# Column mean of 8192 x 8192 floats: first load ahead of the critical section, stores behind it, GpSimd as its leader

## Chip, cores and metric

The kernel runs on one core of one Trainium2 chip. The metric is the device time of one execution in microseconds (us). The core has TensorE (PE), VectorE (DVE), ScalarE (ACT), GpSimd (POOL) and SyncE (SP), each with its own queue of instructions, and 16 DMA engines. Loads and stores are issued from the queues of SP (DMA queue 1) and ScalarE (DMA queue 10).

## Reference

```python
x = np.random.randn(8192, 8192).astype(np.float32)
return np.mean(x, axis=0)          # 8192 column means, float32
```

256 MiB are read and 32 KB written.

## The kernel before

The 8192 rows are 64 slabs of 128 rows, one row of a slab per partition. Two slabs make a pair of 128 x 16384 floats, 64 KB per partition. There are 31 pairs, one more slab ("slab") and a last slab ("last"). Three pair buffers (`bufs`) are used in turn.

Everything stands in one critical section, in which a program orders the engines by its own semaphores and not by the tile framework's. One engine leads a section: at its opening the leader signals the others, which branch into the section's block, and at its end the leader releases them to the closing steps. Before, the leader is SP.

- Loads: `load` issues a DMA. The first pair is loaded from ScalarE's queue in two pieces (columns 0 to 2047, 1 MB, with its own semaphore `first`; then the remaining 7 MB). All others come from SP's queue, in order. Pair 1 waits for `first`, so that the first piece does not share the DMA engines; pair k from 3 on waits until VectorE has read its buffer (`freed`, later a count of `dve`). The last six pairs come in pieces, and the last slab in eight pieces (`PIECES`).
- Sums: VectorE adds, one instruction per half pair (`vadd`, L157): the first half of the new pair takes up the running total, then its second half. 24 pairs are in a loop, the rest is written out. Near the end the pieces get smaller (4096, then 2048 columns).
- Across partitions: TensorE multiplies the total, and the last slab as it lands, by a column of ones (L189), into PSUM banks. Four wide parts of columns (`WIDE`) use four groups of 32 output partitions each, four narrow ones (`NARROW`) one. Eight matmuls on an idle tile (L225) run ahead of them.
- Drains: ScalarE (L248) and VectorE (L251) multiply by 1/8192 and copy from PSUM to `rw`, `r3` and `row`. They count `act` and `dve`.
- Stores: three from SP (L268: the first two wide parts together, the third, the fourth) and one from ScalarE (L282: the 640 narrow columns in `row`). Each waits for a threshold of `act` or `dve`; ScalarE's waits for all of both. Each counts `stored`, and ScalarE ends the section when all four have landed:

```python
        nc.scalar.wait_ge(dve, n_dve)
        nc.scalar.dma_start(out=out[N0:C], in_=row).wait_op(act, n_act, "sem-ge").then_inc(stored, 16)
        nc.scalar.wait_ge(stored, 64)
```

The program's frame adds a barrier of all engines at its start (L298) and at its end (L309). Instructions that the section itself adds have line L94.

Of the kernel before, what the change touches and what calls it, by code (L numbers as in the profile page):

```python
# [7 lines left out]
F32 = mybir.dt.float32  # L8
ADD = mybir.AluOpType.add
MULT = mybir.AluOpType.mult  # L10
P = 128
GROUPS = 4


WIDE = (2048, 2048, 2048, 1408)
NARROW = (192, 288, 96, 64)
PIECES = WIDE + NARROW
FIRST = 2048
# [6 lines left out]
def kernel(  # L25
# [5 lines left out]
    nc = tc.nc  # L31
    R, C = x.shape
    n_slabs = R // P
    n_pairs = n_slabs // 2 - 1
    N0 = sum(WIDE)
# [3 lines left out]
    inv_r = 1.0 / float(R)  # L39

    const_pool = ctx.enter_context(tc.tile_pool(name="const", bufs=1))
    pair_pool = ctx.enter_context(tc.tile_pool(name="pair", bufs=1))
    psum_pool = ctx.enter_context(
        tc.tile_pool(name="acc", bufs=1, space=bass.MemoryType.PSUM)
    )
    res_pool = ctx.enter_context(tc.tile_pool(name="res", bufs=1))

    ones = const_pool.tile([P, 32], F32, name="ones")
    bufs = [pair_pool.tile([P, 2 * C], F32, name=f"pair{b}", tag=f"pair{b}") for b in range(3)]
    banks = [psum_pool.tile([P, 512], F32, name=f"bank{b}", tag=f"bank{b}") for b in range(8)]  # L50
    rw = res_pool.tile([P, 3 * 512], F32, name="rw")
    r3 = res_pool.tile([P, WIDE[3] // GROUPS], F32, name="r3")
    row = res_pool.tile([1, C - N0], F32, name="row")
    idle = res_pool.tile([P, 512], F32, name="idle")

    wide, lo = [], 0
# [19 lines left out]
    def single(n, lo, hi):  # L76
        return blocks[n, :, (RUN - 1) * C + lo : (RUN - 1) * C + hi]

    def source(k, lo, hi):
        if k < n_whole:  # L80
            b, t = divmod(k, RUN // 2)
            return blocks[b, :, 2 * t * C + lo : 2 * t * C + hi]
        j = lo // C
        return single(2 * (k - n_whole) + j, lo - j * C, hi - j * C)

    def cuts(k):
        if k == 0:
            return [(0, FIRST), (FIRST, 2 * C)]
        if k < n_pairs - BY_ROW:
            return [(0, 2 * C)]  # L90
        step = H if k == n_pairs - 1 else C
        return [(lo, lo + step) for lo in range(0, 2 * C, step)]

    with tc.tile_critical():  # L94
        sem = nc.alloc_semaphore
        landed = [sem(f"landed{b}") for b in range(3)]
        first, freed, half = sem("first"), sem("freed"), sem("half")
        dve, act, pe, stored = sem("dve"), sem("act"), sem("pe"), sem("stored")
        came = {}


# [1 line left out]
        for k in range(LOOPED + 1, n_pairs):  # L103
            pair, before = bufs[k % 3], bufs[(k - 1) % 3]
# [18 lines left out]
        def load(key, dst, src, after=None):  # L123

            ld = (nc.scalar if key[0] == 0 else nc.sync).dma_start(out=dst, in_=src)  # L125
            if after is not None:
                ld.wait_op(after[0], after[1], "sem-ge")
            if key not in came:
                came[key] = sem(f"came_{'_'.join(map(str, key))}")
            ld.then_inc(came[key], 16)  # L130

        for k in range(n_pairs):
            for n, (lo, hi) in enumerate(cuts(k)):
                after = None
                if k >= 3 and n == 0:
                    f = k - 3
                    after = (freed, f + 1) if f < LOOPED else (dve, freed_by[f])
                if k == 1:
                    after = (first, 16)
                key = (k, n)  # L140
                if k <= LOOPED:
                    came[key] = first if (k, n) == (0, 0) else landed[k % 3]
                load(key, bufs[k % 3][:, lo:hi], source(k, lo, hi), after)
        r = (n_slabs - 2) * P
        for n in range(2):
# [2 lines left out]
        at, lo = {}, 0  # L148
# [26 lines left out]
        awaited = None  # L175
        for n, (key, a, b) in enumerate(adds):
            if key != awaited:
                nc.vector.wait_ge(came[key], 16)
                awaited = key
# [3 lines left out]
        n_dve = len(adds)  # L183
# [40 lines left out]
        for _ in range(4):  # L224
            nc.tensor.matmul(  # L225
                out=banks[7][:, 0:512], lhsT=idle[:, 0:P], rhs=idle, start=True, stop=True, skip_group_check=True
# [13 lines left out]
            ready["narrow", n] = close(fold_narrow, narrow[n], narrow[n][0])  # L240


        n_act = 0

        def drain(engine, dst, src, awaited):
            nonlocal n_act, n_dve
# [11 lines left out]
        n_r3 = n_dve  # L258
        for n, (engine, part) in enumerate(
            ((nc.scalar, narrow[0]), (nc.vector, narrow[1]), (nc.scalar, ending))  # L260
        ):
            lo, w, g, bank, _ = part
            awaited = ready["narrow", 3 if part is ending else n]
            drain(engine, row[0:1, lo - N0 : lo - N0 + w], bank[g : g + 1, 0:w], awaited)


        def store(lo, hi, src, how, **grouped):
            return nc.sync.dma_start(out=out[lo:hi].rearrange(how, **grouped), in_=src)  # L268

        groups = rw.rearrange("(g r) (n w) -> g r n w", r=32, w=512)[:, 0]  # L270
        at2, at3 = 2 * GROUPS * 512, 3 * GROUPS * 512
        store(0, at2, groups[:, 0:2], "(n g w) -> g n w", g=GROUPS, w=512).wait_op(
            act, 2, "sem-ge"
        ).then_inc(stored, 16)
        store(at2, at3, groups[:, 2], "(g w) -> g w", g=GROUPS).wait_op(act, 3, "sem-ge").then_inc(
            stored, 16
        )
        store(at3, N0, r3.rearrange("(g r) w -> g r w", r=32)[:, 0], "(g w) -> g w", g=GROUPS).wait_op(
            dve, n_r3, "sem-ge"
        ).then_inc(stored, 16)  # L280
        nc.scalar.wait_ge(dve, n_dve)
        nc.scalar.dma_start(out=out[N0:C], in_=row).wait_op(act, n_act, "sem-ge").then_inc(stored, 16)  # L282
        nc.scalar.wait_ge(stored, 64)


# [28 lines left out]
```

## Time and profile before

| | |
|---|---|
| median of 3 runs | 627.33 us (627.28 to 627.36) |
| the profiled execution | 627.58 us |
| its span, first to last instruction | 625.8 us (625.77) |
| DMA queue 1 (SP) and queue 10 (ScalarE), share of 16 engines' span | 96.1% and 3.2% |
| read from memory, rate over the span | 268.44 MB, 429 GB/s |
| VectorE busy | 541.3 us (86%) |
| one addition of 128 x 8192 | 8.69 us |
| granted TensorE clock | 1.000 |

The span runs from the first to the last instruction of the program; the rest of the time lies around it. In the chain of waits a row gives start, length and what the time went to; "SPq" and "ACTq" are instructions that the queue of SP or ScalarE handles itself (branches, semaphore instructions, DRAINs, the issue of a DMA). [...] The trace also has a record for each packet of the DMA engines, with its queue, start, length and bytes, and for each count of a semaphore.

### The profile page before, as it was taken

What the parts mean: (1) busy time and instruction counts of PE and PEld (TensorE: products, weight loads), DVE (VectorE), ACT (ScalarE), POOL (GpSimd) and SP (SyncE); (2) the same over time, 40 slices, a digit from 0 to 9 for tenths busy, and PEclk for the clock granted to TensorE, in tenths of its full rate; (3) what the DMA queues carried; (4) which work ended last, traced back from release to release, by engine and by line L of the source; (5) the groups of instructions that cost most, each with busy time, mean ns of one, the idle gap of its engine ahead of it and who ended that gap; (6) DMA issues with size and microseconds to landing.
All of it is one profiled execution on the core that took longest, in us unless ns stands there. A gap on an engine that the chain in (4) does not pass through costs nothing.

```text
span 625.8 us, 467 instructions
## 1 busy us (share of the span) xinstructions
PE 13.7 (2%) x86; PEld 4.6 (1%) x86; DVE 541.3 (86%) x71; ACT 3.7 (1%) x6; POOL 0.2 (0%) x4
## 2 busy tenths in 40 slices
PE   0000000000000000000000000000000000000025
PEld 0000000000000000000000000000000000000011
DVE  0049999989888899888898888988889899999996
ACT  0000000000000000000000000000000000000001
POOL 0000000000000000000000000000000000000000
PEclk9999999999999999999999999999999999999999
DMA  9999999999999999999999999999999999999997
GB/s 380 433 461 402 469 402 469 402 469 402 469 402 461 411 452 419 448 423 406 465 402 469 402 469 402 469 402 469 402 469 402 434 429 425 431 425 436 435 429 312
DMA packets 7231, 268.48 MB, mean 429 GB/s; under 512 B 1069, under 2 KB 1329, under 8 KB 1470
## 3 DMA queue, kind: packets, MB, share of 16 engines
q1 hardware_dynamic: 6940, 260.08, 96.1%
q10 hardware_dynamic: 290, 8.39, 3.2%
q14 instruction: 1, 0.01, 0.0%
HBM read 268.44 MB, written 0.03 MB: 429 GB/s over the span
## 4 chain that ended last, share of the span: by engine, by line
DMA 59%; DVE 39%; issue 0%; SPq 0%; PE 0%; DVEq 0%; ACTq 0%
DMA pair<-in_x_dram 59%; DVE pair L157 39%; SPq L125 0%; PE bank L189 0%; DVE row L251 0%; ACTq L125 0%; DVEq L170 0%; DVEq L168 0%; DVEq L157 0%; ACTq L309 0%; SPq L94 0%
## 5 line engine op out<-in xcount | busy, mean ns | idle before, releaser
L157 DVE TENSOR_TENSOR pair<-pair 128x8192 f32<-128x8192 f32 (+1 forms) x32 | 269.6, 8426 | 42.4 <-DMA pair<-in_x_dram 38.7
L157 DVE TENSOR_TENSOR pair<-pair,pair 128x8192 f32<-128x8192 f32 (+2 forms) x35 | 270.1, 7717 | 35.5 <-DMA pair<-in_x_dram 35.0
L225 PE MATMUL bank<-idle 128*128 128x512 f32 x8 | 5.3, 818 | 605.5 <-DVE pair L157 605.5
L189 PE MATMUL bank<-pair,ones 128*32 128x512 f32 (+5 forms) x78 | 8.4, 523 | 3.7 <-DVE pair L157 3.6
L225 PEld LDWEIGHTS bank<-idle 128*128 128x128 f32 x8 | 2.1, 276 | 607.9 <-DVE pair L157 605.5
L248 ACT ACTIVATE rw<-bank 128x512 f32<-128x512 f32 x3 | 1.8, 597 | 617.2 <-PE bank L189 617.2
L251 DVE TENSOR_SCALAR r<-bank 128x352 f32<-128x352 f32 x1 | 0.5, 525 | 3.2 <-PE bank L189 3.2
L189 PEld LDWEIGHTS bank<-pair,ones 128*32 128x32 f32 x78 | 2.6, 108 | 10.2 <-DVE pair L157 7.1
L248 ACT ACT_TABLE_LOAD x1 | 1.3, 1283 | 1.8 <-issue 1.8
L159 DVE MEMSET ones<- 128x32 f32 x1 | 0.1, 85 | 1.0 <-SPq L94 1.0
L248 ACT ACTIVATE row<-bank 1x192 f32<-1x192 f32 (+1 forms) x2 | 0.6, 308 | 0.6 <-PE bank L189 0.6
L160 DVE MEMSET idle<- 128x512 f32 x1 | 0.5, 485 | 0.1
L251 DVE TENSOR_SCALAR row<-bank 1x288 f32<-1x288 f32 x1 | 0.4, 449 | 0.0
L298 POOL MEMSET const-bfloat16-1.0<- 128x1 bf16 x1 | 0.1, 102 | 0.0
L298 POOL MEMSET const-uint8-127<- 128x1 uint8 x1 | 0.1, 102 | 0.0
L298 POOL MEMSET const-float32-0.0<- 128x1 f32 x1 | 0.1, 99 | 0.2 <-issue 0.2
L298 POOL MEMSET const-float32-1.0<- 128x1 f32 x1 | 0.1, 99 | 0.0
## 6 DMA issues: line engine op xcount, KB each, us to landing
pair<-in_x_dram SPq DMA_DIRECT2D x10, 4096.0 KB, 27.6
pair<-in_x_dram SPq DMA_DIRECT2D x6, 2048.0 KB, 28.4
pair<-in_x_dram ACTq DMA_DIRECT2D x1, 7168.0 KB, 38.1
pair<-in_x_dram SPq DMA_DIRECT2D x3, 1024.0 KB, 33.4
pair<-in_x_dram ACTq DMA_DIRECT2D x1, 1024.0 KB, 4.7
pair<-in_x_dram SPq DMA_DIRECT2D x1, 704.0 KB, 36.6
pair<-in_x_dram SPq DMA_DIRECT2D x24, 29.8
pair<-in_x_dram SPq DMA_DIRECT2D x1, 144.0 KB, 30.2
```

Of the source, the lines that this page charges most:

```text
L157: return nc.vector.tensor_tensor(out=a, in0=a, in1=b, op=ADD)
L159: nc.vector.memset(ones, 1.0)
L160: nc.vector.memset(idle, 0.0)
L189: return nc.tensor.matmul(out=dst, lhsT=ones, rhs=src, skip_group_check=True, **flags)
L225: nc.tensor.matmul(out=banks[7][:, 0:512], lhsT=idle[:, 0:P], rhs=idle, start=True, stop=True, skip_group_check=True)
L248: op = engine.mul(out=dst, in_=src, mul=inv_r).then_inc(act, 1)
L251: op = engine.tensor_scalar(out=dst, in0=src, scalar1=inv_r, scalar2=None, op0=MULT).then_inc(dve, 1)
L298: nc = _bacc.Bacc("TRN2", target_bir_lowering=False, num_devices=1)
```

## The change

The first load is issued ahead of the critical section, with a semaphore allocated there. Inside the section it is skipped. GpSimd, which has no instruction in the section, leads it in place of SP. The four stores are issued behind the section, with their thresholds put into registers inside it; the semaphore `stored` is gone, and the tile framework gives each store a semaphore of its own, for which SP waits in the program's closing steps. ScalarE's store is preceded by a wait for its own five drains, and itself waits for VectorE's. The pair buffers and `rw`, `r3`, `row` are allocated by hand and no longer from pools, and the access patterns of the moved transfers are given so that the framework adds no dependencies. `heads` writes out the same source pattern as the rearrangement before. In the built programs the first pair buffer lies at byte 16640 of each partition before and at 16512 after, the other buffers behind it.

```diff
-    bufs = [pair_pool.tile([P, 2 * C], F32, name=f"pair{b}", tag=f"pair{b}") for b in range(3)]
+    bufs = [nc.alloc_sbuf_tensor(f"pair{b}", [P, 2 * C], F32).ap() for b in range(3)]
...
-    rw = res_pool.tile([P, 3 * 512], F32, name="rw")
-    r3 = res_pool.tile([P, WIDE[3] // GROUPS], F32, name="r3")
-    row = res_pool.tile([1, C - N0], F32, name="row")
+    rw = nc.alloc_sbuf_tensor("rw", [P, 3 * 512], F32).ap()
+    r3 = nc.alloc_sbuf_tensor("r3", [P, WIDE[3] // GROUPS], F32).ap()
+    row = nc.alloc_sbuf_tensor("row", [P, C - N0], F32).ap()[0:1, :]
...
-    with tc.tile_critical():
-        sem = nc.alloc_semaphore
-        landed = [sem(f"landed{b}") for b in range(3)]
-        first, freed, half = sem("first"), sem("freed"), sem("half")
-        dve, act, pe, stored = sem("dve"), sem("act"), sem("pe"), sem("stored")
+    def untracked(ap, size):
+        return bass.AP(tensor=ap.tensor, offset=ap.offset, ap=ap.ap, dep_tracking_offset=size)
+
+    sem = nc.alloc_semaphore
+    landed = [sem(f"landed{b}") for b in range(3)]
+    first = sem("first")
+
+    early = nc.scalar.dma_start(out=untracked(bufs[0][:, 0:FIRST], 2 * C * P), in_=source(0, 0, FIRST))
+    early.then_inc(first, 16)
+    tc.no_tile_sem_insts.add(early.ins.name)
+
+    wide_act, third_act, last_wide = (nc.sync.alloc_register(n) for n in ("wide_act", "third_act", "last_wide"))
+    all_act, all_dve = (nc.scalar.alloc_register(n) for n in ("all_act", "all_dve"))
+
+    with tc.tile_critical(sync_engine=mybir.EngineType.Pool) as section:
+        tc.declare_no_dep(section, early.ins, reason="awaited by first")
+        freed, half = sem("freed"), sem("half")
+        dve, act, pe = sem("dve"), sem("act"), sem("pe")
...
+                if key == (0, 0):
+                    continue
                 load(key, bufs[k % 3][:, lo:hi], source(k, lo, hi), after)
...
-        n_act = 0
+        n_act, drains = 0, (5, n_dve + 2)
+        nc.scalar.reg_mov(all_act, drains[0])
+        nc.scalar.reg_mov(all_dve, drains[1])
...
-        store(0, at2, groups[:, 0:2], "(n g w) -> g n w", g=GROUPS, w=512).wait_op(
-            act, 2, "sem-ge"
-        ).then_inc(stored, 16)
-        store(at2, at3, groups[:, 2], "(g w) -> g w", g=GROUPS).wait_op(act, 3, "sem-ge").then_inc(
-            stored, 16
-        )
-        store(at3, N0, r3.rearrange("(g r) w -> g r w", r=32)[:, 0], "(g w) -> g w", g=GROUPS).wait_op(
-            dve, n_r3, "sem-ge"
-        ).then_inc(stored, 16)
-        nc.scalar.wait_ge(dve, n_dve)
-        nc.scalar.dma_start(out=out[N0:C], in_=row).wait_op(act, n_act, "sem-ge").then_inc(stored, 16)
-        nc.scalar.wait_ge(stored, 64)
+        for engine, register, value in (
+            (nc.sync, wide_act, 2), (nc.sync, third_act, 3), (nc.sync, last_wide, n_r3)
+        ):
+            engine.reg_mov(register, value)
+
+    def behind(ins, *others):
+        for name in (section.name, *others):
+            tc.add_manual_dep(
+                ins,
+                name,
+                mybir.DependencyInfo(mybir.DependencyClass.NoSync, mybir.DependencyReason.SCHED_ONLY),
+                reason="issued behind",
+            )
+
+    def store(engine, lo, hi, src, awaited, register, how=None, **grouped):
+        dst = out[lo:hi].rearrange(how, **grouped) if how else out[lo:hi]
+        st = engine.dma_start(out=dst, in_=untracked(src, C * P)).wait_op(awaited, register, "sem-ge")
+        behind(st.ins)
+        return st
...
+    store(nc.sync, 0, at2, heads(rw, 0, [[512, 2], [1, 512]]), act, wide_act, "(n g w) -> g n w", g=GROUPS, w=512)
+    store(nc.sync, at2, at3, heads(rw, 1024, [[1, 512]]), act, third_act, "(g w) -> g w", g=GROUPS)
+    wide_st = store(nc.sync, at3, N0, heads(r3, 0, [[1, WIDE[3] // GROUPS]]), dve, last_wide, "(g w) -> g w", g=GROUPS)
+    drained = nc.scalar.nop().wait_op(act, all_act, "sem-ge")
+    behind(drained.ins)
+    behind(store(nc.scalar, N0, C, row, dve, all_dve).ins, drained.ins.name, wide_st.ins.name)
```

In the built program the leader's opening signal and its release of the others follow each other at once on GpSimd, and the closing drain of each engine stands between its last instruction in the section and its stores.

More of the change, by code (lines that the diff above doesn't have):

```diff
@@ L41 @@
     const_pool = ctx.enter_context(tc.tile_pool(name="const", bufs=1))
-    pair_pool = ctx.enter_context(tc.tile_pool(name="pair", bufs=1))
     psum_pool = ctx.enter_context(
@@ L264 @@
             drain(engine, row[0:1, lo - N0 : lo - N0 + w], bank[g : g + 1, 0:w], awaited)
[L267 to L271, printed above, removed]
-        store(0, at2, groups[:, 0:2], "(n g w) -> g n w", g=GROUPS, w=512).wait_op(
-            act, 2, "sem-ge"
-        ).then_inc(stored, 16)
@@ new lines @@
+        assert (n_act, n_dve) == drains
+    def behind(ins, *others):
[11 more added lines that the diff above has]
+        return st
@@ new lines, in heads @@
+    def heads(ap, lo, dims):
+        step = ap.ap[0][0] * P // GROUPS
+        return bass.AP(tensor=ap.tensor, offset=ap.offset + lo, ap=[[step, GROUPS], *dims])
+    at2, at3 = 2 * GROUPS * 512, 3 * GROUPS * 512
+    store(nc.sync, 0, at2, heads(rw, 0, [[512, 2], [1, 512]]), act, wide_act, "(n g w) -> g n w", g=GROUPS, w=512)
+    store(nc.sync, at2, at3, heads(rw, 1024, [[1, 512]]), act, third_act, "(g w) -> g w", g=GROUPS)
+    wide_st = store(nc.sync, at3, N0, heads(r3, 0, [[1, WIDE[3] // GROUPS]]), dve, last_wide, "(g w) -> g w", g=GROUPS)
```

## The prediction

> **What bounds the kernel now.** I read the page first, then the chain of waits in its first two microseconds, then the tail: the timeline from 621.4 us on, and the instructions that belong to the section's own line (L94).
>
> From the page, the busy time by engine, the DMA row of the 40 slices and the queue rows:
>
> ```profile
> PE 13.7 (2%) x86; PEld 4.6 (1%) x86; DVE 541.3 (86%) x71; ACT 3.7 (1%) x6; POOL 0.2 (0%) x4
> ...
> DMA  9999999999999999999999999999999999999997
> ...
> q1 hardware_dynamic: 6940, 260.08, 96.1%
> q10 hardware_dynamic: 290, 8.39, 3.2%
> ```
>
> VectorE is busy 86%, but the DMA engines never stop: queues 1 and 10 fill 99.3% of 16 engines' span. The packet records put it more sharply: from about 4 us until the tail at 622 us all 16 engines have a packet under way, with some hundredths of a microsecond of idle in all. VectorE needs 2 x 8.69 us for a pair of slabs that takes the DMA engines 8.39 MB / 435 GB/s = 19.3 us, so it waits for them. The time is therefore: first packet, plus 268 MB at a fixed rate, plus a tail. An edit can move only the first term and the last, or the rate.
>
> The chain of waits from 0 to 60 us (start, length, what) is the first term:
>
> ```profile
> 0.72 0.01 SPq L94
> 0.73 0.02 issue
> 0.75 0.03 ACTq L309
> 0.78 0.12 issue
> 0.90 0.39 ACTq L125
> 1.28 0.03 issue
> 1.32 38.12 DMA pair<-in_x_dram
> ```
>
> SP opens the section (0.72), ScalarE branches into it (0.75), and 0.15 us after the start of that branch issues the first load (0.90). Its first packet starts at 1.92, 1.02 us behind.
>
> The timeline of the tail is the last term, with the section's end below it (durations in ns, then first and last start):
>
> ```profile
> 622.11 0.56 SPq L268 DMA_DIRECT2D out_dram<-rw  x1
> ...
> 622.97 0.50 SPq L268 DMA_DIRECT2D out_dram<-r  x1
> 622.98 0.45 DVE L251 TENSOR_SCALAR row<-bank 1x288 f32<-1x288 f32 x1
> 623.52 0.58 ACTq L282 DMA_DIRECT2D out_dram<-row  x1
> ```
> ```profile
> L94 SPq DRAIN  x1: 407/407/407, 623.6 to 623.6; - x1
> L94 ACTq COMPARE_BRANCH  x1: 33/33/33, 624.8 to 624.8; - x1
> L94 ACTq DRAIN  x1: 8/8/8, 625.0 to 625.0; - x1
> L94 SPq NOP  x1: 13/13/13, 625.0 to 625.0; - x1
> ```
>
> The row store, issued at 623.518 behind VectorE's last drain (counted at 623.437), lands last: its semaphore is full at 624.778. Then come ScalarE's branch (624.799), its DRAIN (624.955), SP's NOP (624.988) and SP's two drains (625.062, 625.126), before the closing barrier that ends the span at 625.77.
>
> **The change, part by part.** *First load.* It moves in front of the section, so it no longer waits for SP's NOP and ScalarE's branch. SP's NOP stood 0.068 us behind SP's release from the opening barrier (0.648 to 0.716). ScalarE is released at 0.652, so its first load is issued at about 0.72 instead of 0.90: **-0.18 us**. Its queue: the second load (7 MB) now stands behind the branch that the first has left. Issue 0.385, gap 0.03, then 0.148 from branch to issue: 1.28 against 1.316. The first load's packets last until about 4.7 us and the second's could start at 1.28 + 1.02 = 2.3, so 2.4 us of cover remain and the engines do not run dry. SP's first load waits for the first load's landing and comes earlier with it. As nothing between 2 and 622 us leaves an engine idle, the whole stream moves by the 0.18. From 57 us on a buffer comes free 4.2 us or more before the previous load lands (57.02 against 61.24, then 74.59 against 80.59), so no refill becomes late.
>
> *GpSimd as leader.* It has nothing to do in the section. In the built program it opens it with a NOP, adds at once the count for which the others' closing drains wait, and then waits for those drains. Its opening NOP should stand at 0.69, where its first drain is now (SP's: 0.716); only VectorE's and ScalarE's branches follow it, and nothing late hangs on them. Zero. If it were slow, only the second load's 2.4 us of cover would be eaten.
>
> *Stores on SP.* Behind its last load (issued by 604.70) SP gets three register moves, a branch and a drain before the first store. Register moves took 0.05 us on VectorE, a branch about 0.15, and a drain behind a DMA issue 0.407 (above): 0.7 us in all, and the first store waits for ScalarE's second drain until 619.56. Cover 14 us; cost zero, and 0.7 without that cover. The store's three thresholds are the old values (2, 3, and the wide drain), so 619.58, 622.11 and 622.97 stay relative to the stream. A wait on a register is in no row; I take it as a wait on a constant.
>
> *Row store on ScalarE.* It now stands behind a branch, a drain of ScalarE, and a wait for its five activations; it waits for VectorE itself instead of behind an extra wait. ScalarE's last activation is counted at 623.346. GpSimd's drain behind its memsets ended 0.05 us after the last of them and its next wait began 0.044 later; with the 0.06 from a wait to the next issue this gives 623.50 against 623.518: **-0.02 us**. Ends: -0.06 if the drain hides and the store follows VectorE's count at once; +0.36 if ScalarE's drain takes the 0.407 of SP's. I take the first kind, since ScalarE has issued no DMA for 620 us, and SP's long drain came right behind one. Only the row store and the closing barrier queue behind this drain.
>
> *End.* ScalarE no longer collects the stores; SP waits for each store's own count and goes on to the barrier. From the last landing: 0.021 to the wait, then 0.063 to each drain (SP's two waits at 624.076 and 624.139, its drains at 625.062 and 625.126). The second drain stands 0.148 behind the landing instead of 0.348: **-0.20 us**, with 0.15 to 0.25 as ends. ScalarE's closing drain now follows its store directly; SP's ended 0.53 us after such an issue, which is 624.63 against the 624.93 at which SP gets there. Covered by 0.3.
>
> *Addresses.* The buffers leave their pools, and in the built programs the first pair buffer moves from byte 16640 of each partition to 16512, so every load's destination shifts by 128 bytes and no longer lies on a multiple of 256. The packets carry this price, and they are very regular: 8192 bytes take 309 ns, 65536 bytes 2418, so 36.8 ns per KB and about 8 ns for each. Rows with an odd 128 are there: the 384-byte packets start at such an address on both sides and took 22 ns, on the line between 256 (18 ns) and 768 bytes (36 ns); the row store's 2560 bytes leave from one (220800), arrive on a multiple of 256, and took 102, the line's value. I take zero. If each packet paid for a whole leading 256-byte block, it would cost 128 bytes more, 4.6 ns; 6400 load packets on 16 engines are 400 each: +1.84 us. [...]
>
> **Sum.** -0.18 - 0.02 - 0.20 = -0.40 us. The profiled execution took 627.58 (span 625.77 and 1.81 around it), so 627.18 for one like it; the median of the runs stands 0.25 below the profiled one, and 627.33 - 0.40 = 626.93. A change under 0.2% (1.25 us) is about what a measurement of this kernel can tell from no change, and this is 0.06%.
>
> **Rivals.** (1) The earlier load gains nothing: the first packets of a cold start are slow (they took up to 1044 ns where 309 is usual), and the second load moves by 0.03 only. Then 0.15 of the start is lost: 627.08. Against it: the second load is ready long before the first is through.
>
> (2) The destinations' shift changes the packet time: +1.84 - 0.40 = 628.77, slower by 0.23%. The kernel is slower than before from 1.0 ns per packet on (0.40 us over 400), and by over 0.2% from 4.1 (a 65536-byte packet of 2422 for 2418), everywhere in the stream. For it: nothing here had only its destination off. Against: the two rows above. The same shift could help by as much, for which no row speaks.
>
> (3) The closing steps hold the stores up. Either SP's drain waits for the loads to land: SP's three stores would be issued one behind another from 622.6, ending 0.9 us later; with the row store then no longer the last, about +0.7 - 0.40 = 627.63. Against: SP's long drain ended at 624.00, while its last store landed until 624.60. Or ScalarE has to fetch instructions at its branch at 623.0: 1.02 to a first packet, 0.4 for an 8192-byte packet on queue 14 and 0.3 to its landing come to 624.75, so the row store is 1.25 late and the run ends at 628.2. [...] Against it the one fetch in the tail (624.837, 0.399 long) starts as ScalarE's branch ends, yet ScalarE's drain follows at 624.955, before it is over.
>
> **How the numbers follow.** Forecast 0.72, rival 1 0.09, rival 3 0.05: all three within 0.2%, 0.86. Rival 2 0.09 slower, 0.05 in the helpful direction. Range: low end -0.18 - 0.06 - 0.25, and 0.25 for the distance between two occasions (the profile's own): 626.6; high end no start gain, +0.36, -0.15 and some of that distance: 627.7. Rival 2 and the fetch stay outside.
>
> **What would show it.** First load at about 0.72 and first packet about 1.74; packets of 65536 bytes still at 2418 ns; first store about 0.2 before 619.58; row store at about 623.3; closing barrier 0.15 behind the last landing instead of 0.35. A 65536-byte packet off by 4 ns or more, or engines idle before 622 us, would make the forecast wrong.

## The result, and the profile after

The changed kernel takes 628.38 us (median of 22 runs, 628.25 to 628.97) against 627.58 (22 runs, 627.28 to 628.18): the ratio is 1.0012, 95% interval 1.0007 to 1.0018. It is slower by 0.8 us where 0.4 faster was forecast, and lies outside the range (626.6 to 627.7). The profiled execution took 628.97, the slowest of the 22, with a span of 627.13, 1.36 more than before.

The three edges of the program did what was forecast. The chain of waits of the changed kernel from 0 to 60 us (start, length, what):

```profile
0.73 0.39 ACTq L102
1.11 0.04 issue
1.16 0.03 ACTq L345
1.19 0.11 issue
1.30 38.04 DMA pair<-in_x_dram
```

The first load is issued at 0.73 (forecast 0.72; before 0.90), its first packet starts at 1.742 (1.917). The branch and the second load stand behind it, at 1.16 and 1.30.

The end, in the timeline from 622 us on, and below it the section's own line L109 from 620 us on (durations in ns, then first and last start):

```profile
623.30 0.56 SPq L304 DMA_DIRECT2D out_dram<-rw  x1
...
624.52 0.50 SPq L304 DMA_DIRECT2D out_dram<-r  x1
624.53 0.45 DVE L269 TENSOR_SCALAR row<-bank 1x288 f32<-1x288 f32 x1
625.05 0.58 ACTq L304 DMA_DIRECT2D out_dram<-row  x1
```
```profile
L109 PEldq DRAIN  x1: 465/465/465, 624.1 to 624.1; - x1
L109 DVEq DRAIN  x1: 531/531/531, 624.5 to 624.5; - x1
L109 ACTq DRAIN  x1: 352/352/352, 624.6 to 624.6; - x1
L109 POOLq NOP  x1: 13/13/13, 625.2 to 625.2; - x1
```

ScalarE's drain is 352 ns long, but it starts at 624.568, while the last activation still has to run, and ends 0.034 us behind it (VectorE's, begun at 624.492, ends 0.046 behind its row of L269 above); the row store follows VectorE's last drain by 0.074 us where it was 0.091. SP's drain took 7 ns, at 606.1, and no branch stands behind SP's last load or in ScalarE's tail. The closing steps of SP (line L345, from 626.0 to 626.6):

```profile
L345 SPq EVENT_SEMAPHORE  x2: 28/28/28, 626.1 to 626.3; - x2
L345 SPq DRAIN  x2: 7/7/7, 626.4 to 626.5; - x2
```

The last store has landed at 626.315, and the second of these drains stands at 626.459: 0.144 behind, where it was 0.348.

What grew is the stream between these edges. The page of the changed kernel shows the DMA engines as full as before:

```profile
DMA  9999999999999999999999999999999999999997
...
DMA packets 7231, 268.48 MB, mean 428 GB/s; under 512 B 1069, under 2 KB 1329, under 8 KB 1470
...
q1 hardware_dynamic: 6940, 260.08, 96.2%
```

The same 7231 packets, at 428 GB/s for 429. The DMA issues show where that is (size of each, median us from issue to landing). Before:

```profile
pair<-in_x_dram SPq DMA_DIRECT2D x10, 4096.0 KB, 27.6
pair<-in_x_dram SPq DMA_DIRECT2D x6, 2048.0 KB, 28.4
...
pair<-in_x_dram SPq DMA_DIRECT2D x3, 1024.0 KB, 33.4
```

After:

```profile
pair<-in_x_dram SPq DMA_DIRECT2D x10, 4096.0 KB, 27.8
pair<-in_x_dram SPq DMA_DIRECT2D x6, 2048.0 KB, 28.9
...
pair<-in_x_dram SPq DMA_DIRECT2D x3, 1024.0 KB, 33.9
```

By these medians the late loads take longer in each group. The packet records show why. Before, all 1280 packets of 32768 bytes take 1213 ns, all 768 of 16384 take 611, and all 384 of 8192 bytes on queue 1 take 309. After, they take 1213 to 1222, 611 to 621 and 309 to 321, with means of 1216.9, 614.8 and 313.4: 3.8 to 4.4 ns more on the average, at each of the three sizes. That is the forecast's rival 2. In the profiled execution the stages of the stream answer for the 1.36 us (a stage runs from the first packets of one size to the first of the next, on the average of the 16 engines; the 65536-byte stage counts from the very first packet, and the small packets are those from 5632 bytes down): start -0.18, 65536-byte stage +0.82, 32768 +0.32, 16384 +0.18, 8192 +0.10, small packets +0.14, from the last load packet to the span's end -0.02. Most of the +0.82 is not typical: in the second profile of this kernel, below, that stage is 0.29 longer than before.

### The profile page after: what moved, and what is told of

The parts are those of the page before. It is cut to its first block, busy times and chain, and to the rows that moved or that the text cites. A ratio compares the mean times of both kernels' runs of the same rounds, so it can differ in the third digit from the quotient of the medians.

```text
span 627.1 us, 475 instructions
## 1 busy us (share of the span) xinstructions
PE 14.7 (2%) x86; PEld 4.8 (1%) x86; DVE 541.3 (86%) x71; ACT 3.7 (1%) x6; POOL 0.2 (0%) x4
## 2 busy tenths in 40 slices
DMA packets 7231, 268.48 MB, mean 428 GB/s; under 512 B 1069, under 2 KB 1329, under 8 KB 1470
## 4 chain that ended last, share of the span: by engine, by line
DMA 59%; DVE 39%; issue 0%; SPq 0%; DVEq 0%; PE 0%; ACTq 0%
DMA pair<-in_x_dram 59%; DVE pair L173 39%; SPq L139 0%; PE bank L205 0%; DVE r L269 0%; DVEq L109 0%; ACTq L102 0%; DVEq L186 0%; DVEq L184 0%; DVEq L173 0%; ACTq L345 0%; DVEq L194 0%
## 5 line engine op out<-in xcount | busy, mean ns | idle before, releaser
L173 DVE TENSOR_TENSOR pair<-pair 128x8192 f32<-128x8192 f32 (+2 forms) x67 | 539.7, 8055 | 79.1 <-DMA pair<-in_x_dram 74.8
L269 DVE TENSOR_SCALAR r<-bank 128x352 f32<-128x352 f32 x1 | 0.5, 525 | 3.5 <-PE bank L205 3.5
L269 DVE TENSOR_SCALAR row<-bank 1x288 f32<-1x288 f32 x1 | 0.4, 448 | 0.0
```

What stands on the lines that cost most here:

```text
L173: return nc.vector.tensor_tensor(out=a, in0=a, in1=b, op=ADD)
L269: op = engine.tensor_scalar(out=dst, in0=src, scalar1=inv_r, scalar2=None, op0=MULT).then_inc(dve, 1)
```

## The experiments

The theory was that the destinations, which no longer lie on a multiple of 256 bytes, make each load packet dearer (A). Against it stood that the moved transfers or the new section disturb the stream (B), and that the profiled execution was odd (C).

**The shift alone.** The kernel before, with the small tile `ones` allocated behind the pair buffers:

```diff
-    const_pool = ctx.enter_context(tc.tile_pool(name="const", bufs=1))
     pair_pool = ctx.enter_context(tc.tile_pool(name="pair", bufs=1))
+    const_pool = ctx.enter_context(tc.tile_pool(name="const", bufs=1))
```

> The kernel before with one thing changed: the small tile of ones is allocated behind the pair buffers, so that these start at byte 16512 of a partition and not at 16640, as in the changed kernel. Loads, stores and section are untouched. Theory A (a destination off a multiple of 256 bytes makes every load packet dearer): load packets some 4 ns longer on the average (32768 bytes: 1217 for 1213), stream longer by 400 x 4 ns = 1.6 us, time slower than before by 1.2 to 1.8 us, first load still issued at 0.90. Theory B (the moved load and stores, or the new section's edges, disturb the stream): packets and time as before, within 0.2 us. Theory C (the profiled execution of the changed kernel was an odd one, and addresses mean nothing): packets as before.

Measured: 628.75 (11 runs) against 627.65 (33 runs) of the kernel before on the same chip, ratio 1.0017 (1.0008 to 1.0026). The packets have the changed kernel's lengths (32768 bytes: 1213 to 1224, mean 1217.0), and the loads take as long as there; the DMA issues of this kernel:

```profile
pair<-in_x_dram SPq DMA_DIRECT2D x10, 4096.0 KB, 27.8
pair<-in_x_dram SPq DMA_DIRECT2D x6, 2048.0 KB, 28.9
```

Only the places of `ones` and of the pair buffers were changed, and VectorE is busy as long as before (541.2 us for 541.3), so B and C fall: the shift costs 1.1 us. By stages against the profile of before: 32768 +0.32, 16384 +0.18, 8192 +0.10, small packets +0.11, 65536 +0.35, tail +0.15, together the 1.20 by which the span is longer. The tail is the time from the last load packet to the span's end, and its part is a new one: the semaphore count of the last slab's fourth wide piece (packets of 5632 bytes) is full 0.48 us after its last packet's end, where it was 0.32 (0.51 in the changed kernel), and TensorE's last matmuls wait for it.

The 65536-byte stage needs a closer look, since a few of its packets are slow, with any buffers. With the packets over 2430 ns set aside (36 to 269 of 3072 in an execution), the others average 2418.5 to 2418.6 ns in all seven profiles with aligned buffers (this section's and that of before), and 2420.0 to 2421.0 in all six with shifted ones: 1.4 to 2.5 ns each, over 192 packets per engine. So these packets pay too, 0.3 to 0.5 us in all.

**The change without the shift.** The changed kernel with a pad of 128 bytes per partition ahead of the pair buffers:

```diff
+    nc.alloc_sbuf_tensor("pad", [P, 32], F32)
     bufs = [nc.alloc_sbuf_tensor(f"pair{b}", [P, 2 * C], F32).ap() for b in range(3)]
```

> The changed kernel with a 128-byte pad ahead of the pair buffers, so that they start at byte 16640 as before. Theory A: load packets back at 1213 (32768 bytes) and 309 (8192), and the -0.40 us of the edges left over: 0.3 to 0.5 us faster than before, span about 625.4. Theory B: as slow as the changed kernel, 0.8 us slower than before. Theory C: no difference from the changed kernel in the same call.

Measured: 627.47 against 627.65, ratio 0.9994 (0.9985 to 1.0003), profiled span 625.81. Every packet of 32768, 16384 and 8192 bytes (queue 1) is back at 1213, 611 and 309. From the DMA issues of this kernel:

```profile
pair<-in_x_dram SPq DMA_DIRECT2D x10, 4096.0 KB, 27.6
pair<-in_x_dram SPq DMA_DIRECT2D x6, 2048.0 KB, 28.4
```

A again. The gain left over, 0.18 us, is less than the 0.3 to 0.5 expected, and the interval includes no change.

**The changed kernel again**, on the same chip:

> The changed kernel again, on the chip of the other runs of this call. Both A and B: 0.7 to 1.4 us slower than before, 32768-byte packets at 1217 on the average. Theory C: packets at 1213 and time within 0.4 us of before.

Measured: 628.54, ratio 1.0013 (1.0004 to 1.0022), 32768-byte packets 1217.1 on the average. It stands 1.07 over the padded one and 0.21 under the shifted one. So the three edges bring about 0.2 us with either place of the buffers, by the medians, where 0.40 was forecast; the intervals, of about 0.6 us to each side, can't tell 0.2 from 0.4 or from nothing.

**A multiple of 512.** The kernel before with 256 bytes ahead of `ones`:

```diff
+    pad = const_pool.tile([P, 64], F32, name="pad")
     ones = const_pool.tile([P, 32], F32, name="ones")
```

> The kernel before with a 256-byte pad ahead of the buffers, so that they start at byte 16896, a multiple of 512. Theory A in the form that 256 bytes is the step: same as before within 0.2 us, packets 1213. A in the form that a coarser step counts too: packets shorter by up to 4 ns, up to 1.6 us faster. B and C: same as before.

Measured: 627.73, ratio 0.9999 (0.9990 to 1.0008); packets 1213, 611, 309. Being on a multiple of 512 brings nothing beyond a multiple of 256.

**Other distances.** The same pad with 16 floats puts the buffers 64 bytes past a multiple of 256; with 48 floats it puts them 192 past.

```diff
+    pad = const_pool.tile([P, 16], F32, name="pad")   # the second kernel: 48
     ones = const_pool.tile([P, 32], F32, name="ones")
```

> The kernel before, pair buffers at byte 16704 of a partition (64 past a multiple of 256, where the shifted kernel was 128 past). If a packet pays for the bytes between the 256-byte boundary below and its start (theory A1): 64 bytes, 2.3 ns at the packets' slope, so 32768 bytes take about 1215 on the average and the time is 0.6 us over before. If any start off 256 costs the same few ns (A2): 1217 and 0.9 to 1.2 us over, as with the 128-byte shift. If only a start off 128 matters, or 64 is enough (A3): 1213 and as before.

> The same with the buffers at byte 16832, 192 past a multiple of 256. A1: 192 bytes, 6.9 ns, 32768 bytes at 1220 and 1.6 to 2 us over before. A2: 1217 and 0.9 to 1.2 us over. A3, if 64 is enough: as before.

Measured: 628.84 and 628.81 against 627.70, ratio 1.0019 (1.0010 to 1.0028) for each. 32768-byte packets average 1216.8 in both, 8192-byte ones 313.5 and 313.6. So it is the second form: at 32768 bytes, 64 and 192 bytes off cost 3.8 ns and 128 off 3.9 to 4.1. The price is not that of the bytes between the multiple of 256 below and the start: 192 off costs the same 3.8 ns as 64 off.

**Which side.** In both kernels the sources of the pairs and of the single slab are moved by 128 bytes; in the first the destinations are off too (by the edit of the shift alone, not shown again), in the second not. Other columns are summed then, so these two kernels do not return the mean:

```diff
-            return blocks[b, :, 2 * t * C + lo : 2 * t * C + hi]
+            return blocks[b, :, 2 * t * C + lo + 32 : 2 * t * C + hi + 32]
...
-        return blocks[n, :, (RUN - 1) * C + lo : (RUN - 1) * C + hi]
+        return blocks[n, :, (RUN - 1) * C + lo - 32 : (RUN - 1) * C + hi - 32]
```

> The shifted kernel (buffers 128 past a multiple of 256) with the sources shifted too: pairs are read 32 columns further on, the single slabs 32 columns earlier, so other columns are summed; the last slab's reads stay. Both sides of each large load then start 128 past a multiple of 256. If the difference of the two sides is what costs (A4): packets of 32768 bytes back at 1213, time as before but for the last slab's eight pieces. If the destination's start alone costs (A5): 1217, 0.9 to 1.2 us over before. If each side costs for itself: 1221, 2 us over.

> The kernel before with the same shift of the sources alone, destinations on multiples of 256 (other columns are summed). A4: 1217 on the average and 0.9 to 1.2 us over before. A5: as before, 1213. Each side for itself: 1217, 0.9 to 1.2 us over.

Measured: 628.81 with both sides off, ratio 1.0019 (1.0010 to 1.0028); 627.49 with the sources alone off, 0.9998 (0.9989 to 1.0007). Their DMA issues, both off and then source off:

```profile
pair<-in_x_dram SPq DMA_DIRECT2D x10, 4096.0 KB, 27.8
pair<-in_x_dram SPq DMA_DIRECT2D x6, 2048.0 KB, 28.9
```
```profile
pair<-in_x_dram SPq DMA_DIRECT2D x10, 4096.0 KB, 27.6
pair<-in_x_dram SPq DMA_DIRECT2D x6, 2048.0 KB, 28.4
```

Of these two sides, the destination's start alone counts. Off sources leave every packet of 32768 bytes at 1213, and matching the two sides brings nothing.

**The edges one by one**, on aligned buffers. First the padded kernel again, then the first load alone moved ahead of the section, then all but that. The first diff is against the kernel before, the second against the changed kernel; in both the buffers are allocated by hand behind the pad of 128 bytes:

> The changed kernel with its buffers back on a multiple of 256, once more, since its gain of 0.18 us was inside the interval. If the three edge terms hold (theory E): 0.3 to 0.45 us faster than before, first load issued at 0.73, span's end 3.46 us behind the last load packet where before has 3.65. If they do not reach the time (theory F): within 0.1 us of before.

> The kernel before with one part of the change: the first load issued ahead of the section (buffers allocated by hand at byte 16640, as before); SP leads, stores stay in the section. E: first load at 0.73 for 0.90, first packet at 1.74 for 1.92, tail as before (3.65 from the last load packet to the span's end), 0.17 us faster. F, if the stream's start does not matter: first packet 1.74 and the last load packet where it was.

```diff
+    early = nc.scalar.dma_start(out=untracked(bufs[0][:, 0:FIRST], 2 * C * P), in_=source(0, 0, FIRST))
+    early.then_inc(first, 16)
+    tc.no_tile_sem_insts.add(early.ins.name)
...
-    with tc.tile_critical():
+    with tc.tile_critical() as section:
+        tc.declare_no_dep(section, early.ins, reason="awaited by first")
...
+                if key == (0, 0):
+                    continue
```

> The changed kernel at byte 16640 with its first load back inside the section: GpSimd leads, stores behind the section. E: first load at 0.86 to 0.90, first packet about 1.9, tail 3.45 to 3.5, 0.2 us faster than before; the second drain of SP 0.15 behind the last landing. F: tail 3.65 as before.

```diff
-    early = nc.scalar.dma_start(out=untracked(bufs[0][:, 0:FIRST], 2 * C * P), in_=source(0, 0, FIRST))
-    early.then_inc(first, 16)
-    tc.no_tile_sem_insts.add(early.ins.name)
...
-        tc.declare_no_dep(section, early.ins, reason="awaited by first")
...
-                if key == (0, 0):
-                    continue
```

Measured against 627.64 (27 runs): padded 627.47, ratio 0.9996 (0.9987 to 1.0005); first load alone 627.76, 1.0000 (0.9991 to 1.0009); all but it 627.50, 0.9997 (0.9988 to 1.0006). No interval excludes no change. From the records of the profiled executions, in us:

| | first packet | 65536-byte stage | of it slow packets | last load packet to span's end | span |
|---|---|---|---|---|---|
| before | 1.917 | 484.02 | 0.27 | 3.65 | 625.77 |
| buffers on 512 | 1.911 | 483.75 | 0.03 | 3.66 | 625.51 |
| sources alone off | 1.912 | 483.78 | 0.05 | 3.63 | 625.51 |
| padded | 1.740 | 484.32 | 0.58 | 3.47 | 625.81 |
| padded again | 1.750 | 484.36 | 0.61 | 3.50 | 625.82 |
| first load alone | 1.747 | 484.32 | 0.52 | 3.64 | 625.99 |
| all but first load | 1.906 | 484.45 | 0.60 | 3.48 | 626.24 |

The slow packets are those over 2430 ns, and their column has what they take beyond 2418 ns, on the average of the 16 engines.

The edges are there, each in the kernels that have it and in no other: 0.17 at the first packet, 0.15 to 0.18 at the end. But the 65536-byte stage differs by up to 0.7 us between executions of kernels with equal destinations, more than both edges together. Nearly all of that is slow packets: without them the stage takes 483.72 to 483.86 us in these seven, with the early first load and without it (484.07 to 484.27 in the six with shifted buffers). So the early start is kept to the end of the stage, and slow packets can hide it. What makes them slow is open. Of these seven, the profiled executions with the least (buffers on 512, sources alone off) were the fastest of their 11 runs, and that of "all but first load", with 0.60, the slowest of its 11. All three with the early first load have over 0.5, but so has that one without it, and the changed kernel has 0.76 in one profile and 0.04 in the other. So whether the early load brings slow packets is not settled, and the median of the kernel with that edge alone shows no gain. That the stores' edge reaches the time is what its row says, since nothing follows it; the runs alone could not show it.

## Why the prediction was wrong

- **Address term: the step that failed.** "I take zero" for the buffers' move by 128 bytes. It measures +1.1 us (the shift alone) and turned the sign. The dear alternative, 4.6 ns per packet (4.7 by its own slope, whose 36.8 ns are for 1000 bytes), was nearly right in size: 3.6 to 4.4 was measured at 5632 to 32768 bytes, over 160 packets per engine, 0.6 us; 1.4 to 2.5 at 65536 bytes, 0.3 to 0.5 us; the later landing in the tail adds the rest. Rival 2 put the slowdown at 1.44 us (+1.84 - 0.40) where 0.80 came, since it had all 400 packets pay in full. No run shows the whole leading block of 256 bytes that it was worked out from: 64, 128 and 192 bytes off cost 3.8 to 4.1 ns on 32768 bytes alike.
- **Why zero was taken: two rows read for more than they said.** The 384-byte packet, at 22 ns with an off destination, is too small to show the price: the change puts it on a multiple of 256, and it still takes 22. In the changed kernel 256-byte packets with off destinations still take 18 ns and 124 of 128 packets of 768 bytes take 36, while 5632 bytes take 218.6 on the average for 215. And the row store's 2560 bytes were off on the source side alone, and off sources cost the loads nothing (32768 bytes stayed at 1213). "Nothing here had only its destination off", says rival 2, and yet that case got 0.09.
- **First load: right as far as it was sized.** -0.17 at the issue and at the first packet, for -0.18. "The whole stream moves by the 0.18" holds for the 65536-byte stage with slow packets set aside; that it reaches the time is not shown (rival 1's time stays possible, though not its reason, since the stage does not grow by the 0.15).
- **Second load, GpSimd as leader, SP's steps: right** that they cost nothing. The second load is issued at 1.30 (forecast 1.28), GpSimd's opening NOP stands at 0.69, and SP's drain takes 7 ns, where 0.407 us was allowed.
- **Row store: right**, -0.017 for -0.02, though not by its path: no branch stands in ScalarE's tail, and the drain hides, so neither the +0.36 end nor the fetch of rival 3 occurs: the drain ends 0.034 us behind the last activation, and the one packet of the instruction queue (14) in the tail starts at 626.292, 1.24 us behind the issue of the row store (625.051).
- **End: right**, 0.144 from landing to drain for the 0.148 forecast.
- **A term that was missing**: the landing of the last slab's fourth wide piece, +0.16 to 0.23 in the kernels with off destinations.
- **The base**: 627.33 was the median of 3 runs; 22 runs give 627.58, so the 0.25 between that median and the profiled execution came from the low times of those three. It does not touch the difference of 0.8 us.

## What to carry to other kernels

When a change moves buffers, look at the addresses before and after: here buffers that lay 128 bytes lower, off a multiple of 256, cost more than three well-placed edits at the edges could bring. In a stream without a gap every nanosecond per packet counts by the number of packets (here 400 per engine), so keep the destinations of large loads on multiples of 256 bytes: off them a packet of 32768 bytes took 3.8 to 4.1 ns more here, on them (buffers at 16640 and 16896) each took 1213. A row that looks like the missing case has to agree with it in size and in side before it may stand for zero.

## What was not expected of the hardware

An off destination costs about the same for 64, 128 and 192 bytes (3.8 to 4.1 ns on 32768 bytes), and an off source nothing (1213). Packets up to 768 bytes pay nothing or next to nothing (256 and 768 bytes average 18.0 and 36.1 ns in the changed kernel, for 18 and 36), with one exception: 384-byte packets average 24.8 for 22 in the kernel at 192, where they start 64 past a multiple. At 1152 bytes 51 becomes 53. The cost is not even: on each of the 16 engines the changed kernel's packets of 32768 bytes run through a row of lengths between 1213 and 1222 that repeats after 32 packets, nearly to the nanosecond, where aligned ones are 1213 without exception. What in the engine makes that row was not tried.
